# Attention in a hybrid diffusion layer: where the softmax sums' reciprocals are multiplied in

## The chip, the cores and the metric

The kernel runs on one core of a Trainium2 chip. The time is what the device needs for one execution of the whole program (two layers), in microseconds (us); lower is better. The time shown is the median of three runs. Beside it stands one profiled execution, whose trace gives the start and the duration of each instruction. TensorE does the matrix products, VectorE (DVE in the rows) the elementwise work with two operands and the reductions, ScalarE (ACT) the activations and copies, GpSimd (POOL) a few subtractions, SyncE (SP) issues most DMAs.

## The reference

Two layers over 512 latent tokens and 256 context tokens of width 1024: layer 0 mixes tokens by attention and a short convolution, layer 1 by a state-space scan; each is followed by a feed-forward block. What the change touches is the attention of layer 0, with 8 heads:

```python
def _attend(qn, qr, kn, kr, v):
    s = einsum('bqhd,bkhd->bhqk', qn, kn) + einsum('bqhr,bkr->bhqk', qr, kr)
    p = softmax(s.astype(float32) * MLA_SCALE, axis=-1).astype(v.dtype)
    return einsum('bhqk,bkhd->bqhd', p, v)
```

Latent queries see all 768 keys, context queries the 256 context keys. A value vector has 64 numbers. Everything is float32.

## The kernel before, in words

To keep float32 accuracy with TensorE's fast format (float32r), an operand is split into a rounded part (hi) and the rest (lo). A product of two such operands is three matrix products (hi·hi, hi·lo, lo·hi; the helper `mm3`).

The attention works on 24 units: 8 heads times 3 parts. Parts 0 and 1 are 256 latent queries each against 768 keys, part 2 is the 256 context queries against 256 keys. Per unit there are two functions.

`scores(h, part, q)` (lines 743 to 763): TensorE makes the scores of two tiles of 128 queries into three PSUM banks. VectorE takes the negated row maxima (line 755, one reduction over both tiles). ScalarE takes the exponentials with that as bias, and their row sums (line 758). VectorE takes the sums' reciprocals `ri`, two columns of 128 numbers (line 760), and then multiplies each tile of exponentials by its column, in place (line 762, seen in the trace at the helper's line 107).

`values(h, part, p)` (lines 765 to 793): in three steps (one for part 2), TensorE transposes four 128x128 pieces of `p` into one of two PSUM banks (`tr`, line 139), ScalarE copies them as hi into a ring of three SBUF buffers (line 783), VectorE writes the rest as lo (line 784), and TensorE multiplies the values with hi and lo into the bank `po` (lines 788 and 789). `V` holds hi and lo of the values side by side, so `po` has the hi part in partitions 0 to 63 and the lo part in 64 to 127. At the end ScalarE copies the lower half of `po` to SBUF, and VectorE adds the two halves into `m32`:

```python
t = O32()
self.act(t[0:64], po[64:128], AF.Copy)
self.tt(m32[sl, part * 256:(part + 1) * 256], po[0:64], t[0:64], ALU.add)
```

`po` is a ring with a single place, PSUM bank 5: the value products of the next unit write the same bank. `m32` gathers two heads, and is split again for the output projection (lines 812 to 814).

The loop (lines 801 to 815) makes the scores two units ahead: while `values` of unit u runs, `scores` of unit u+2 is under way. In between stand the projection of the next head's queries (`q_head`, line 732, whose VectorE part is a product of 128x768) and of the keys of the next two heads. The order of instructions on each engine is not written by hand: a planner lays out the program by its own timeline of what is ready when, and on the chip each engine then works through its queue in that order. Semaphores hold an instruction until what it reads is written and what it overwrites has been read. After the attention come the splits of the convolution's results, the output projection (line 864 on) and the feed-forward block.

Of the kernel before, what the change touches and what calls it, by code (L numbers as in the profile page):

```python
# [11 lines left out]
AF = mybir.ActivationFunctionType  # L12
ALU = mybir.AluOpType
# [80 lines left out]
class Kern:  # L94
# [358 lines left out]
    def mixer0(self):  # L453
# [12 lines left out]
        m32 = b(NT)  # L466
# [108 lines left out]
        for f in range(8):  # L575
# [10 lines left out]
            if f in (3, 4):  # L586
                t = f + 1
# [83 lines left out]
        t = tmp()  # L671
# [5 lines left out]
        for e in range(2):  # L677
            sl = slice(64, 128) if e == 0 else slice(0, 64)
# [6 lines left out]
        for j in range(4):  # L685
# [5 lines left out]
            u = tmp()  # L691
# [14 lines left out]
        PS, PQ, PO, PTp = Ring(psa, [0], 1536), Ring(psa, [1536], NT), Ring(psa, [2560], 512), Ring(psa, [3072, 3584], 512)  # L706
# [12 lines left out]
        def key_proj(p):  # L719
            w = self.loadw(io["uk"][p], 256, WK)  # L720
            ps = PQ()
            self.gemm_fm(ps, w, ck, nk=2)
            k32 = K32()
            self.act(k32, ps, AF.Copy)
            return k32

        def key_rows(k32, e):
            sl = slice(0, 64) if e == 0 else slice(64, 128)
            self.act(Kp[e][0][sl], k32[sl], AF.Copy)
            self.tt(Kp[e][1][sl], k32[sl], Kp[e][0][sl], ALU.subtract, eng=nc.gpsimd)  # L730

        def q_head(h):
            w = self.loadw(io["uq"][h], 384, WQ)
            ps = PQ()
            self.gemm_fm(ps, w, cq, nk=3)
            q32 = Q32()
            self.tt(q32, ps, Geff[h % 2], ALU.mult)
            q = Q()
            self.act(q[:, :NT], q32, AF.Copy)
            self.tt(q[:, NT:], q32, q[:, :NT], ALU.subtract, eng=nc.gpsimd)  # L740
            return q[:, :NT], q[:, NT:]

        def scores(h, part, q):

            kp = Kp[h % 2]
            n = NT if part < 2 else NC
            ps = PS(2 * n)
            for i in range(2):
                t = 2 * part + i
                a = [q[j][:, t * 128:(t + 1) * 128] for j in range(2)]  # L750
                for c0, c1 in (SEGS if i == 0 else SEGS[::-1]) if part < 2 else (CTX,):
                    o = i * n + (c0 - (NT - n) if i == 0 or part == 2 else (c0 - NL if c0 else NC))
                    self.mm3(ps[:, o:o + c1 - c0], a, [kp[j][:, c0:c1] for j in range(2)], True, True)
            nm, sm, ri = self.small(2), self.small(2), self.small(2)
            nc.vector.tensor_reduce(out=nm, in_=ps.rearrange("p (i n) -> p i n", i=2), axis=AX.X, op=ALU.max, negate=True)
            p = Pr(2 * n)
            for i in range(2):
                self.act(p[:, i * n:(i + 1) * n], ps[:, i * n:(i + 1) * n], AF.Exp, bias=nm[:, i:i + 1],
                         accum_out=sm[:, i:i + 1])
            nc.vector.reciprocal(ri, sm)  # L760
            for i in range(2):
                self.ts(p[:, i * n:(i + 1) * n], p[:, i * n:(i + 1) * n], ri[:, i:i + 1])
            return p

        def values(h, part, p):
            n = NT if part < 2 else NC
            po = PO(256)
            kts = range(6) if part < 2 else (4, 5)

            def col(i, kt):  # L770

                if part == 2:
                    return i * n + (kt - 4) * 128
                return i * n + (kt * 128 if i == 0 else ((kt - 4) * 128 if kt >= 4 else NC + kt * 128))
            for kk in range(0, len(kts), 2):
                pt = PTp()
                for k in range(2):
                    for i in range(2):
                        c = col(i, kts[kk + k])
                        self.tr(pt[:, k * 256 + i * 128:k * 256 + (i + 1) * 128], p[:, c:c + 128])  # L780
                hl = PT()
                hi, lo = hl[:, :512], hl[:, 512:]
                self.act(hi, pt, AF.Copy)
                self.tt(lo, pt, hi, ALU.subtract)
                for k in range(2):
                    kt = kts[kk + k]
                    v = V[kt][:, h * 128:(h + 1) * 128]
                    self.mm(po, v, hi[:, k * 256:(k + 1) * 256], kt == kts[0], False)
                    self.mm(po, v, lo[:, k * 256:(k + 1) * 256], False, kt == kts[-1])
            t = O32()  # L790
            sl = slice(0, 64) if h % 2 == 0 else slice(64, 128)
            self.act(t[0:64], po[64:128], AF.Copy)
            self.tt(m32[sl, part * 256:(part + 1) * 256], po[0:64], t[0:64], ALU.add)

        k32 = key_proj(0)
        qs = {0: q_head(0)}
# [1 line left out]
        key_rows(k32, 1)  # L798
        units = [(h, part) for h in range(8) for part in range(3)]
        prob = {u: scores(0, u, qs[0]) for u in range(2)}  # L800
        for u, (h, part) in enumerate(units):
            if part == 0 and h + 1 < 8:
                qs[h + 1] = q_head(h + 1)
            if part == 1 and h % 2 == 1 and h < 7:
                k32 = key_proj((h + 1) // 2)
                key_rows(k32, 0)
            if u + 2 < len(units):
                prob[u + 2] = scores(*units[u + 2], qs[units[u + 2][0]])
            if part == 1 and h % 2 == 1 and h < 7:
                key_rows(k32, 1)  # L810
            values(h, part, prob.pop(u))
            if part == 2 and h % 2 == 1:
                self.act(mixA[0][h // 2], m32, AF.Copy)
                self.tt(mixA[1][h // 2], m32, mixA[0][h // 2], ALU.subtract, eng=nc.gpsimd)
                self.tap("attn", m32, h // 2)
# [862 lines left out]
```

## Time and profile before

| | |
|---|---|
| Time, median of 3 runs | 1946.99 us (1946.28 to 1947.25) |
| Profiled execution: its own time | 1947.97 us |
| Profiled execution: span from first to last instruction | 1946.2 us, 25422 instructions |
| TensorE busy | 1840.2 us (95%) |
| VectorE busy | 1285.7 us (66%) |
| ScalarE busy | 865.3 us (44%) |
| GpSimd busy | 472.2 us (24%) |
| Mean granted TensorE clock | 0.982 of 2.4 GHz |

The profiled execution's own time is 1.8 us longer than its span (what lies before the first and behind the last instruction), and 1.0 us longer than the median of the runs. In a row of the trace, `128x768 f32<-128x768 f32 x32 | 25.6, 843` means 32 instructions with this output and input, 25.6 us busy in all and 843 ns each in the mean. In a timeline, a row begins with start and duration in us, instructions of one kind that follow each other are merged (x4), and a bracket gives the idle time of the engine just before and what ended it. TensorE's matrix products overlap in its pipeline: one that lasts 272 ns can follow the one before it after 109 ns.

### The profile page before, as it was taken

The numbers are of one execution on the slowest core, as the hardware profiler recorded it, in microseconds if no ns is written. First come the engines' busy times: TensorE is split into PE (matmuls) and PEld (weight loads), VectorE is DVE, ScalarE is ACT, GpSimd is POOL, SyncE is SP. The second block draws the span as 40 slices with busy tenths as digits, with TensorE's granted clock in tenths as the row PEclk, the third lists the DMA queues.
The fourth block names the chain that finished last, engine by engine and source line by source line (L and its number), as shares of the span: only waits on it lengthen the run. The fifth ranks groups of instructions, "written<-read, shape, count | busy, mean of one in ns | idle before, by whom it ended". The sixth has DMA issues, their size and how long they took to land. (4 is left out here: it accounts for less than half of the span.)

```text
span 1946.2 us, 25422 instructions
## 1 busy us (share of the span) xinstructions
PE 1840.2 (95%) x9752; PEld 1549.7 (80%) x9752; DVE 1285.7 (66%) x1859; ACT 865.3 (44%) x1346; POOL 472.2 (24%) x578
## 2 busy tenths in 40 slices
PE   7999998889999999999978999999999899999997
PEld 3787787778888888888857887887778788888886
DVE  3332378746999988767666688877776266555564
ACT  4422376645534334334444556565562254333332
POOL 1000124112011111111151367777674110000002
PEclk9899999999999999999998999999999999999999
DMA  8145300153888989877662434444477963223222
GB/s 320 61 153 178 95 25 12 34 174 108 291 307 314 331 325 350 303 257 241 235 252 92 171 124 158 152 168 169 144 262 291 351 214 105 76 97 98 98 87 76
DMA packets 84034, 355.13 MB, mean 182 GB/s; under 512 B 10828, under 2 KB 13320, under 8 KB 66760
## 3 DMA queue, kind: packets, MB, share of 16 engines
q1 hardware_dynamic: 67560, 264.63, 38.0%
q0 software_dynamic: 16352, 88.87, 13.3%
q8 instruction: 77, 1.26, 0.3%
q14 instruction: 45, 0.37, 0.1%
HBM read 277.28 MB, written 76.18 MB: 182 GB/s over the span
## 5 line engine op out<-in xcount | busy, mean ns | idle before, releaser
L131 PE MATMUL psum<-arena_r 128*128 128x512 f32 (+1 forms) x8876 | 1752.8, 357 | 47.8 <-DVE arena_f L113 14.6
L131 PEld LDWEIGHTS psum<-arena_r 128*128 128x128 f32 x8876 | 1466.5, 190 | 306.6 <-ACT arena_r L101 21.9
L113 DVE TENSOR_TENSOR arena_r<-arena_f,arena_r 128x512 fp32r<-128x512 f32 (+5 forms) x417 | 388.6, 948 | 278.2 <-ACT arena_r L101 276.1
L101 ACT ACTIVATE arena_r<-arena_f 128x1024 fp32r<-128x1024 f32 (+5 forms) x465 | 344.7, 765 | 432.4 <-PE psum L131 151.0
L113 POOL TENSOR_TENSOR arena_f<-arena_f 128x256 f32<-128x256 f32 (+6 forms) x344 | 323.6, 966 | 200.2 <-ACT arena_f L101 83.0
L101 ACT ACTIVATE arena_f<-arena_f 128x512 f32<-128x512 f32 (+7 forms) x203 | 160.5, 806 | 274.0 <-DMA ws_dram<-arena_f 101.3
L110 DVE SCALAR_TENSOR_TENSOR arena_f<-psum,arena_f 128x511 f32<-128x511 f32 (+1 forms) x356 | 217.9, 649 | 64.6 <-ACT arena_f L101 61.4
L113 DVE TENSOR_TENSOR arena_f<-psum,arena_f 64x256 f32<-64x256 f32 (+6 forms) x277 | 174.8, 647 | 99.5 <-PE psum L131 82.8
L101 ACT ACTIVATE arena_f<-psum,arena_f 128x768 f32<-128x768 f32 (+2 forms) x201 | 153.6, 771 | 112.8 <-PE psum L131 58.8
L113 DVE TENSOR_TENSOR arena_f<-arena_f 128x512 f32<-128x512 f32 (+5 forms) x189 | 161.3, 865 | 48.5 <-ACT arena_f L101 33.1
L107 POOL TENSOR_SCALAR arena_f<-arena_f 128x1 f32<-128x1 f32 (+2 forms) x88 | 34.1, 388 | 558.4 <-ACT junk L101 455.9
L204 POOL DMA_DIRECT2D ws_dram<-arena_f x57 | 31.3, 548 | 459.3 <-DVE arena_f L113 361.4
L139 PE MATMUL psum<-arena_f 128*128 128x128 f32 x596 | 96.4, 285 | 45.5 <-DVE arena_f L107 30.2
L101 ACT ACTIVATE arena_f<-psum 128x512 f32<-128x512 f32 (+9 forms) x152 | 80.7, 549 | 105.2 <-PE psum L131 91.9
L139 PEld LDWEIGHTS psum<-arena_f 128*128 128x128 f32 x596 | 71.3, 143 | 64.6 <-DVE arena_f L107 35.9
L113 POOL TENSOR_TENSOR arena_r<-arena_f,arena_r 128x768 fp32r<-128x768 f32 (+2 forms) x28 | 50.1, 1803 | 247.2 <-ACT arena_r L101 232.5
L110 DVE SCALAR_TENSOR_TENSOR arena_f<-arena_f 128x512 f32<-128x512 f32 (+4 forms) x107 | 70.9, 701 | 53.7 <-ACT arena_f L101 45.3
L317 DVE SCALAR_TENSOR_TENSOR junk<-arena_f 128x1024 bf16<-128x1024 f32 x80 | 97.5, 1219 | 1.9 <-DMA arena_f<-in_mod_t_dram 1.5
L101 ACT ACT_TABLE_LOAD x51 | 65.4, 1283 | 34.6 <-DVE arena_f L110 18.8
L107 DVE TENSOR_SCALAR arena_f<-arena_f 128x512 f32<-128x512 f32 (+4 forms) x97 | 55.2, 612 | 29.2 <-POOL arena_f L113 28.5
L101 ACT ACTIVATE arena_r<-psum 128x512 fp32r<-128x512 f32 (+2 forms) x72 | 41.1, 591 | 28.2 <-PE psum L139 14.3
L113 DVE TENSOR_TENSOR arena_r<-psum,arena_r 128x512 fp32r<-128x512 f32 (+2 forms) x72 | 47.4, 674 | 9.0 <-ACT arena_r L101 8.7
(29 smaller groups left out, 300.6 us busy)
## 6 DMA issues: line engine op xcount, KB each, us to landing
arena_r<-ws_dram SPq DMA_DIRECT2D x64, 1024.0 KB
ws_dram<-arena_f POOLq DMA_DIRECT2D x56, 1024.0 KB, 5.2
arena_f<-in_ffn_up_dram SPq DMA_DIRECT2D x88, 512.0 KB
arena_f<-in_mod_t_dram SPq DMA_DIRECT2D x56, 512.0 KB
arena_f<-in_ffn_down_dram SPq DMA_DIRECT2D x44, 512.0 KB
arena_f<-in_mod_dram SPq DMA_DIRECT2D x40, 512.0 KB
arena_f<-a_dram SPq DMA_DIRECT2D x32, 512.0 KB
arena_f<-in_ssd_w_dram POOLq DMA_DIRECT2D x24, 512.0 KB, 7.1
```

The costliest lines, as they stand in the source:

```text
L101: return self.nc.scalar.activation(out=out, in_=in_, func=func, **kw).ins
L107: (eng or self.nc.vector).tensor_scalar(**kw)
L110: self.nc.vector.scalar_tensor_tensor(out=out, in0=in0, scalar=s, in1=in1, op0=op0, op1=op1)
L113: return (eng or self.nc.vector).tensor_tensor(out=out, in0=a, in1=b, op=op).ins
L131: self.nc.tensor.matmul(out, a, b, start=start, stop=stop)
L139: self.nc.tensor.transpose(out, in_, self.ident)
L204: g.dma_start(out=self.wsd[i * 128:(i + 1) * 128, :2 * n], in_=hl)
L317: self.nc.vector.scalar_tensor_tensor(out=self.junk2, in0=r, scalar=1.0, in1=self.cb[c], op0=ALU.mult, op1=ALU.mult, accum_out=o)
```

## The change

`scores` no longer multiplies the exponentials by `ri`; it hands `ri` on. `values` multiplies the exponentials as they are. Behind the value products, TensorE makes two more products per unit, in float32 (not float32r): a column of `ri`, repeated 64 times as the stationary operand, times the 128x128 identity. This writes `ri` of 128 queries as a row, on 64 partitions, into the second half of the bank `po` (columns 256 to 511). The sum of the two halves of the value product now goes to SBUF, and another VectorE instruction of 64x256 multiplies it by these rows into `m32`.

```diff
             nc.vector.reciprocal(ri, sm)
-            for i in range(2):
-                self.ts(p[:, i * n:(i + 1) * n], p[:, i * n:(i + 1) * n], ri[:, i:i + 1])
-            return p
+            return p, ri
 
-        def values(h, part, p):
+        def values(h, part, p, ri):
             n = NT if part < 2 else NC
-            po = PO(256)
+            po = PO(512)
...
-                    self.mm(po, v, hi[:, k * 256:(k + 1) * 256], kt == kts[0], False)
-                    self.mm(po, v, lo[:, k * 256:(k + 1) * 256], False, kt == kts[-1])
+                    self.mm(po[:, :256], v, hi[:, k * 256:(k + 1) * 256], kt == kts[0], False)
+                    self.mm(po[:, :256], v, lo[:, k * 256:(k + 1) * 256], False, kt == kts[-1])
+            for i in range(2):
+                self.mm(po[0:64, 256 + i * 128:256 + (i + 1) * 128], ri[:, i:i + 1].to_broadcast([128, 64]), self.ident, True, True)
             t = O32()
             sl = slice(0, 64) if h % 2 == 0 else slice(64, 128)
-            self.act(t[0:64], po[64:128], AF.Copy)
-            self.tt(m32[sl, part * 256:(part + 1) * 256], po[0:64], t[0:64], ALU.add)
+            self.act(t[0:64], po[64:128, :256], AF.Copy)
+            self.tt(t[0:64], po[0:64, :256], t[0:64], ALU.add)
+            self.tt(m32[sl, part * 256:(part + 1) * 256], po[0:64, 256:], t[0:64], ALU.mult)
...
-            values(h, part, prob.pop(u))
+            values(h, part, *prob.pop(u))
```

## Rows read from the trace of the kernel before

**Rows 1.** The page: busy time of each engine over the whole span, share and instructions.

```profile
PE 1840.2 (95%) x9752; PEld 1549.7 (80%) x9752; DVE 1285.7 (66%) x1859; ACT 865.3 (44%) x1346; POOL 472.2 (24%) x578
```

**Rows 2.** Three stretches of the attention: start and end and length in us, then busy us and instructions of TensorE's products, its weight loads, VectorE, ScalarE and GpSimd, the granted TensorE clock, the DMA share and GB/s.

```profile
235.00:295.00 60.00, 57.09 (x369) 50.37 (x368) 46.13 (x74) 39.98 (x81) 17.85 (x10) 1.00 0.09 29
295.00:394.00 99.00, 83.43 (x547) 71.71 (x545) 80.33 (x123) 65.44 (x138) 28.16 (x16) 1.00 0.10 29
315.00:375.00 60.00, 49.86 (x331) 43.09 (x329) 53.54 (x76) 42.39 (x89) 22.84 (x13) 1.00 0.06 19
```

**Rows 3.** What TensorE's products waited for between 235 and 394 us: tile and line, us in total, times, longest.

```profile
PE psum L139 <- DVE arena_r L113: 6.1, 8, 1.5
PE psum L131 <- DVE arena_f L113: 4.5, 4, 1.3
PE psum L139 <- DVE arena_f L107: 3.3, 3, 1.5
PE psum L131 <- DVE arena_r L113: 3.1, 3, 1.4
```

**Rows 4.** VectorE between 235 and 394 us, by line and shape: busy us, mean ns, and the idle time before.

```profile
L755 DVE TENSOR_REDUCE arena_f<-psum 128x2 f32<-128x1536 f32 x16 | 28.0, 1751 | 1.7 <-PE psum L131 1.5
L107 DVE TENSOR_SCALAR arena_f<-arena_f 128x768 f32<-128x768 f32 x32 | 25.6, 843 | 0.4
L113 DVE TENSOR_TENSOR arena_f<-psum,arena_f 64x256 f32<-64x256 f32 x24 | 9.9, 414 | 3.9 <-ACT arena_f L101 3.5
L107 DVE TENSOR_SCALAR arena_f<-arena_f 128x256 f32<-128x256 f32 x16 | 8.8, 593 | 0.1
```

**Rows 5.** TensorE over the whole span, by line and shape (arena_r holds float32r, arena_f float32): busy us, mean ns of one, idle time before.

```profile
L131 PE MATMUL psum<-arena_r 128*128 128x512 f32 x5724 | 1370.1, 395 | 24.1 <-DMA arena_r<-ws_dram 8.4 <-ACT arena_r L101 6.8 <-DVE arena_f L113 6.2
L131 PE MATMUL psum<-arena_r 128*128 128x256 f32 x3056 | 425.9, 288 | 23.8 <-DVE arena_f L113 8.4 <-DVE arena_r L113 7.7 <-ACT arena_r L101 3.9
L131 PE MATMUL psum<-arena_f 128*128 128x512 f32 x2 | 1.0, 590 | 0.0
L131 PE MATMUL psum<-arena_f 128*128 128x256 f32 x2 | 0.6, 378 | 0.0
```

**Rows 6.** Timeline of VectorE and TensorE around 302 us: a reduction of two tiles' scores, and transposes with what they wait for.

```profile
301.26 1.74 DVE L755 TENSOR_REDUCE arena_f<-psum 128x2 f32<-128x1536 f32 x1
302.17 0.60 PE L139 MATMUL psum<-arena_f 128*128 128x128 f32 x4
303.66 0.66 PE L139 MATMUL psum<-arena_f 128*128 128x128 f32 x4 [0.89 <-DVE arena_r L113]
```

**Rows 7.** Timeline around 327 us: the multiplications of line 107, GpSimd beside them, and TensorE.

```profile
325.37 2.71 DVE L107 TENSOR_SCALAR arena_f<-arena_f 128x768 f32<-128x768 f32 x2
325.79 3.99 POOL L113 TENSOR_TENSOR arena_r<-arena_f,arena_r 128x768 fp32r<-128x768 f32 x2 [0.74 <-ACT arena_r L101]
328.13 0.55 PE L139 MATMUL psum<-arena_f 128*128 128x128 f32 x3 [1.44 <-DVE arena_f L107]
```

**Rows 8.** Timeline around 307 us: the same multiplications with GpSimd idle, and TensorE, waiting for the lo part that follows them.

```profile
306.20 1.14 DVE L107 TENSOR_SCALAR arena_f<-arena_f 128x768 f32<-128x768 f32 x2
308.00 0.66 PE L139 MATMUL psum<-arena_f 128*128 128x128 f32 x4 [0.59 <-DVE arena_r L113]
```

**Rows 9.** Six more of TensorE's waits between 236 and 394 us, from its timeline in order of time.

```profile
272.51 0.66 PE L139 MATMUL psum<-arena_f 128*128 128x128 f32 x4 [0.64 <-DVE arena_r L113]
297.18 0.65 PE L139 MATMUL psum<-arena_f 128*128 128x128 f32 x4 [0.70 <-DVE arena_r L113]
323.17 1.55 PE L131 MATMUL psum<-arena_r 128*128 128x256 f32 x10 [1.22 <-DVE arena_f L113]
352.34 0.74 PE L131 MATMUL psum<-arena_r 128*128 128x256 f32 x4 [1.33 <-DVE arena_r L113]
368.77 0.75 PE L131 MATMUL psum<-arena_r 128*128 128x256 f32 x4 [1.43 <-DVE arena_r L113]
392.06 0.73 PE L131 MATMUL psum<-arena_r 128*128 128x256 f32 x4 [1.33 <-DVE arena_f L113]
```

**Rows 10.** VectorE's timeline at three places, around 271, 294 and 321 us: multiplications, a lo part (128x512), and the sum of the two halves (64x256).

```profile
270.11 1.15 DVE L107 TENSOR_SCALAR arena_f<-arena_f 128x768 f32<-128x768 f32 x2
271.77 0.68 DVE L113 TENSOR_TENSOR arena_r<-psum,arena_r 128x512 fp32r<-128x512 f32 x1
...
291.42 2.84 DVE L107 TENSOR_SCALAR arena_f<-arena_f 128x256 f32<-128x256 f32 x2
...
316.68 3.12 DVE L107 TENSOR_SCALAR arena_f<-arena_f 128x768 f32<-128x768 f32 x2
322.69 0.42 DVE L113 TENSOR_TENSOR arena_f<-psum,arena_f 64x256 f32<-64x256 f32 x1
```

**Rows 11.** VectorE's timeline from 349 to 367 us: the first and the last of three places (at 349, 355 and 366 us) at which the sum of the two halves stands ahead of a reduction of 128x1536 and this ahead of lo parts.

```profile
349.48 0.42 DVE L113 TENSOR_TENSOR arena_f<-psum,arena_f 64x256 f32<-64x256 f32 x1
349.93 1.76 DVE L755 TENSOR_REDUCE arena_f<-psum 128x2 f32<-128x1536 f32 x1
...
...
366.36 1.76 DVE L755 TENSOR_REDUCE arena_f<-psum 128x2 f32<-128x1536 f32 x1
```

**Rows 12.** The end of the attention: the last sum, and TensorE, which starts on it.

```profile
393.56 0.42 DVE L113 TENSOR_TENSOR arena_f<-psum,arena_f 64x256 f32<-64x256 f32 x1
394.03 1.47 PE L131 MATMUL psum<-arena_r 128*128 128x512 f32 x3 [1.24 <-DVE arena_f L113]
```

## The prediction

> **What bounds the kernel now.** I read the page first: TensorE is busy 95% of the span [rows 1], so a change in a stage counts only by what it adds to TensorE's queue or takes from its waits. The change lies between 235 and 394 us. In that stage the clock is 1.00 throughout, so nothing is to be had from it, and it has two halves [rows 2]. From 235 to 295 us TensorE is busy 57.1 of 60 us, 95%, with VectorE at 46.1 of 60, 77%. From 315 to 375 us VectorE has risen to 53.5 of 60, 89%, and TensorE fallen to 49.9, 83%. The waits name the partner: all 17.0 us that TensorE's products wait in the stage (6.1 + 4.5 + 3.3 + 3.1) are waits for VectorE [rows 3]. So there is something to win, 17 us at the utmost, 0.9% of the time.
>
> The kind of wait matters more. Three waits, 3.3 us, are for the removed multiplications themselves (line 107) [rows 3]: one is 1.44 us, where two multiplications beside a busy GpSimd take 2.71 us [rows 7] and not 1.14 us as with GpSimd idle [rows 8]. Eleven waits, 9.2 us, are for a lo part (6.1 + 3.1) [rows 3], and what the lo part itself queued behind must be read from VectorE's timeline. Sometimes it is a multiplication [rows 8]; oftener it is the row maxima's reduction, 1.74 us: at 302 us TensorE has filled both transpose banks, the lo part that would free one starts only when the reduction that began at 301.26 ends, and TensorE stands 0.89 us [rows 6]. The reduction stays.
>
> **The change part by part.**
>
> Removed: 32 multiplications of 128x768 (25.6 us) and 16 of 128x256 (8.8 us), 34.4 us of VectorE [rows 4]. Off TensorE's waits this takes: the three for line 107, 3.3 us; the two lo waits that stand right behind multiplications, 0.64 us at 272 and 0.59 us at 308 [rows 8 to 10]. That is 4.5 us, and I count it whole. At two more places multiplications stand further up the chain. Before 323 us 3.12 us of them push two lo parts, these a reduction, and it the sum for which TensorE waits 1.22 us; at 297 us it waits 0.70 us behind such a chain, which begins with 2.84 us [rows 9, 10]. The reduction cannot begin before its scores are made, so I take half of these 1.92 us, 1.0 us. Sum: -5.5 us. The lower bound is the 3.3 us alone; the upper one all of the 17 us.
>
> Added to TensorE: 48 products of 128 columns with 64 stationary columns, in plain float32. The trace has none of this shape. By the rows for float32r, 256 more columns cost 395 - 288 = 107 ns; for float32 590 - 378 = 212 ns [rows 5]: two clocks of 2.4 GHz per column where float32r takes one. So 128 columns need 107 ns. The transposes, also float32 with 128 columns, follow each other after (0.60 - 0.27)/3 = 0.11 us, four in 0.60 us with a last one of 0.27 us [rows 6]. I take 0.11 us each, 0.22 us per unit, 5.3 us for 24 units. Nothing says that a stationary operand which repeats one column loads slower. Bounds: nothing where TensorE would stand anyway, and twice the price if such a load is as slow as a float32 product of 256 columns (215 ns), 10.5 us.
>
> What of the 5.3 us is hidden: where a lo part is held up by a reduction that already runs, 0.22 us more on TensorE ends inside the wait. Of the eleven lo waits two go with the multiplications; I count the nine others, most of which stand behind a reduction, with 0.22 us each, 2.0 us. The other 3.3 us are on the path: in the first half TensorE is 95% busy, and a product there is paid in full. The two products also stand ahead of ScalarE's copy of half of `po`, if the bank is guarded as a whole, and behind that copy in ScalarE's queue wait the next hi parts; these depend on transposes that TensorE issues behind the two products anyway, so this is the same 0.22 us and not a second one. The products wait for `ri`, which has been ready for the better part of two units.
>
> Added to VectorE: 24 multiplications of 64x256 with one operand in PSUM. The sum of the halves has this shape and takes 414 ns [rows 4], so 24 x 0.414 = 9.9 us; VectorE is relieved of 34.4 - 9.9 = 24.5 us net. On the path this instruction counts in two ways. First, `po` is now read 0.41 us longer, and the next unit's value products wait for it: TensorE waits for the sum three times, first at 323 and last at 392 us [rows 9], and three times 0.41 is 1.2 us. Secondly, behind the sum in VectorE's queue stands a reduction and behind that the lo part that TensorE awaits; that is so three times, ahead of the first wait at 352 and of the last at 368 us [rows 9, 11], again 1.2 us. In the other units the multiplication falls into VectorE's own slack. Bounds: nothing, and all 9.9 us.
>
> At the end of the attention copy, sum and output projection follow each other with TensorE idle 1.24 us [rows 12]; the last unit's 0.22 + 0.41 us come on top there. The 0.22 is in the 3.3; I add 0.4 us.
>
> Sum: -5.5 + 3.3 + 1.2 + 1.2 + 0.4 = +0.6 us. No DMA is added, removed or passed, and what follows the attention is TensorE's own queue, so a shift at 394 us is handed on to the end. Against the profiled execution's own 1947.97 us this gives 1948.6; the runs' median is 1.0 us lower, so 1947.6. The halves and shares in this sum are worth some 3 us either way, and VectorE's net relief of 24.5 us, which I have booked only at named waits, leans to the faster side: I put the forecast at 1947.0 us, no change. Its own range is 1943.5 to 1950.5.
>
> **A rule that speaks against the change.** By the rows a float32 product takes two clocks per column [rows 5]. The Trainium skill, page "FP8 and Floating Point Precision", section "TensorE Precision Notes", says that true float32 takes four passes through the array. By that the 48 products would cost 48 x 0.213 = 10.2 us instead of 5.3. The trace does not agree with it for the two shapes that it has, and the sum goes by the trace.
>
> **The rivals.**
>
> *Faster: VectorE is what sets the pace of the second half.* Then the relief is not worth single waits but the pace: with VectorE back below 77% TensorE works the second half as densely as the first. From 295 to 394 us it is busy 83.4 of 99 us [rows 2]; 14 units add 14 x 0.22 = 3.1; at 95.2% this takes 90.9 us, 8.1 less. The first ten units lose 10 x 0.22 = 2.2. That makes -5.9 us, 1941.1. For it: all waits name VectorE, and GpSimd stretches the multiplications most in this half [rows 2, 7]. Against: the reduction, 1.75 us each and 16 times [rows 4], stays in the same queue ahead of the lo parts.
>
> *Slower: the end of a unit becomes the chain.* Two products, copy, sum and multiplication must be over before the next unit's value products may write `po`, and the reduction queues behind them. If that decides in 12 of 24 units, the multiplication costs 12 x 0.41 = 5.0, the products are paid in full, 5.3, and the gain is the same -5.5: +4.8 us, 1951.8. It decides from about ten units on. For it: TensorE already waits for the sum, and a bank with one place leaves no way around. Against: only three such waits in 24 units (the fourth wait for VectorE's arena_f at line 131 is for a head's queries) [rows 3, 9].
>
> *Slower: the new products cost twice.* If repeated columns load slowly, or this shape takes four clocks per column, TensorE gets 10.5 us, and the sum is 0.6 + 5.2 = +5.8 us, 1952.8. The rows speak against it [rows 5].
>
> That the change does not do what it says I leave out: the instructions are plainly removed and added. What is open is the planner: with other durations it orders the stage anew, which can move any of these waits by a microsecond or two; this widens the ranges.
>
> **How the numbers follow.** What a measurement of this kernel can tell from no change is about 0.2%, 3.9 us. Chances: forecast 0.46, faster rival 0.31, end of the unit 0.18, dear products 0.05. The forecast's range lies within 3.9 us of the time before, so the chances are faster 0.31, same 0.46, slower 0.23. The range reaches into both sides: down to 1939.0, two below the faster rival (of the 17 us all but a few could go), up to 1954.0, where both slower cases with some of the planner's own are inside.
>
> **What would show it.** In the trace after, line 107 is gone between 235 and 394 us, and TensorE has no wait for it; that stage's VectorE busy time falls by about 24 us. The two products show as pairs 0.11 us apart. Right is the forecast if the lo waits behind reductions remain, about 8 us, and waits for the new multiplication at `po` appear. Wrong on the fast side: TensorE's busy share from 315 to 375 us rises to 95%. Wrong on the slow side: waits of the value products for VectorE's 64x256 in ten units or more, or pairs 0.2 us apart and more.

## The result and the profile after

The change makes the kernel slower by 0.6%: 1959.26 us in the median (1955.01 to 1962.57, four runs) against 1947.12 us (1946.28 to 1948.58) beside it, a ratio of 1.0059, 95% interval 1.0046 to 1.0071. That is 12.1 us, outside the range of 1939 to 1954. The profiled execution after is the quickest of the four, 1955.01 us, so its trace can show only some 7 us of the loss.

The first line of the page after answers to [rows 1]:

```profile
PE 1851.2 (95%) x9848; PEld 1554.1 (80%) x9848; DVE 1265.5 (65%) x1835; ACT 869.9 (45%) x1350; POOL 471.4 (24%) x578
```

TensorE has 11.0 us and 96 instructions more, where 48 products were added. The same three stretches of the attention as in [rows 2], with the same columns:

```profile
235.00:295.00 60.00, 57.55 (x375) 50.09 (x374) 38.76 (x60) 37.80 (x78) 13.55 (x8) 1.00 0.09 27
295.00:394.00 99.00, 93.53 (x614) 79.27 (x613) 60.55 (x103) 64.30 (x135) 28.66 (x17) 1.00 0.07 22
315.00:375.00 60.00, 56.73 (x374) 47.78 (x372) 39.80 (x66) 40.79 (x85) 20.87 (x13) 1.00 0.06 18
```

VectorE is at 38.8 and 60.6 us in the first two, before at 46.1 and 80.3; TensorE is at 94% of the second, before at 84%, and at 95% from 315 to 375 us, which the prediction had named as the sign of a faster kernel. The stage still ends later: busier TensorE here means more work, not the same work done sooner. What TensorE waited for from 235 us to 402 us, where the attention and its tail now end (tile and line; us, times, longest), answers to [rows 3]:

```profile
PE psum L131 <- DVE arena_f L113: 5.8, 5, 1.5
PE psum L131 <- DVE arena_r L113: 3.4, 4, 1.4
PE psum L131 <- ACT arena_f L101: 0.7, 2, 0.4
PE psum L139 <- DVE arena_r L113: 0.6, 2, 0.3
PE psum L131 <- ACT arena_r L101: 0.3, 1, 0.3
```

The sum is 10.8 us against 17.0. Line 107 is gone, the waits for a lo part (arena_r) fell from 9.2 to 4.0 us, those for arena_f (the sum, now with the multiplication behind it, and a head's queries) rose from 4.5 to 5.8. VectorE by shape in that stretch, for [rows 4]:

```profile
L755 DVE TENSOR_REDUCE arena_f<-psum 128x2 f32<-128x1536 f32 x16 | 28.0, 1753 | 8.3 <-PE psum L131 8.1
L113 DVE TENSOR_TENSOR arena_f<-psum,arena_f 64x256 f32<-64x256 f32 x48 | 20.0, 416 | 10.0 <-ACT arena_f L101 9.1
```

The multiplication costs what the sum does, 416 ns. The reduction had waited 1.7 us for its scores in all and now waits 8.3: VectorE is ahead of TensorE. And the new products, by shape from 235 to 402 us:

```profile
L131 PE MATMUL psum<-arena_f 128*64 128x128 f32 x96 | 15.6, 285 | 0.0
```

and in two places of TensorE's timeline:

```profile
308.55 0.65 PE L131 MATMUL psum<-arena_f 128*64 128x128 f32 x4
309.13 0.66 PE L139 MATMUL psum<-arena_f 128*128 128x128 f32 x4
...
315.05 0.65 PE L131 MATMUL psum<-arena_f 128*64 128x128 f32 x4
315.63 4.69 PE L131 MATMUL psum<-arena_r 128*128 128x512 f32 x25
```

A unit asks for two products; TensorE executes four instructions, and the next one starts 0.58 us after the first (309.13 - 308.55, 315.63 - 315.05). One by one, the starts follow after 0.159, 0.109, 0.109 and 0.203 us (medians of the 24 units).

To see where along the program the time goes, I cut each trace at TensorE's own products, what an edit added not counted: the start of the 1000th (attention), the 2400th (first feed-forward block), the 5250th (scan layer), the 8250th (second feed-forward block). Lengths of before and differences to them, in us, for all kernels:

```
                       start  attention  ffn0   scan   ffn1
before                 185.2    264.4   532.1  607.6  338.4
after                   -3.4     +6.1     0.0   +4.2    0.0
e1_no_products          -3.4     +0.9     0.0   +6.2    0.0
e2_rows_by_transpose    -1.6     -0.7     0.0   +0.1    0.0
e3_products_twice       -2.3    +14.3     0.0   +3.6    0.0
e4_products_only        -1.8    +17.6     0.0   +9.3    0.0
e5_relief_only          -3.5     -3.2     0.0   +6.7    0.0
e6_rows_own_bank        -0.5    +11.0     0.0   -1.1    0.0
e7_barrier_before       -0.8      0.0     0.0   +6.0    0.0
e8_barrier_after        -0.2     +6.0     0.0   +9.0    0.0
e9_before_nudged        -2.6     +0.2    +0.4   +0.6    0.0
e10_after_nudged        -3.0     +5.9     0.0   +1.6    0.0
e11_scale_on_gpsimd     -2.4    +13.2    +2.2   -4.3    0.0
```

The start, which no edit touches, differs from one execution to the next by up to 3.5 us; the granted clock of the first 100 us is 0.93 in the mean before and 0.95 after, which may be part of it. The change costs +6.1 us in the attention and, some 500 us later, +4.2 us in the scan layer, where not one instruction was edited. e9 and e11 have 4 and 20 idle transposes in the first feed-forward block, which are its +0.4 and +2.2.

How far may such a column be trusted? In the attention, TensorE works through its instructions in e7 and e9 in the order of before, in e8 and e10 in the order of after: 0.0 and +0.2, +6.0 and +5.9 beside +6.1, so the same order repeats within 0.2 us. Every other kernel has its own order there, since the planner lays out the stage anew. e2 is closest to after, with 56 of the 1400 products moved (by line, tiles and shape; counted as the fewest that must move); between before and after it is 165, and e1, e3, e4, e5, e6 and e11 are 128 to 229 away from the kernel that they edit. Of the experiments on the attention, e2 is thus the cleanest; the others change the order along with what they are meant to change.

### The profile page after: what moved, and what is told of

Same layout as the page of the kernel before. It is cut to its first block, busy times and chain, and to the rows that moved or that the text cites. A ratio compares the mean times of both kernels' runs of the same rounds, so it can differ in the third digit from the quotient of the medians.

```text
span 1953.2 us, 25617 instructions
## 1 busy us (share of the span) xinstructions
PE 1851.2 (95%) x9848; PEld 1554.1 (80%) x9848; DVE 1265.5 (65%) x1835; ACT 869.9 (45%) x1350; POOL 471.4 (24%) x578
## 4 chain that ended last, share of the span: by engine, by line
PE 40%; issue 20%; DVE 9%; DMA 4%; POOL 3%; ACT 3%; SPq 0%; DVEq 0%; POOLq 0%; ACTq 0%
PE psum L131 39%; DVE arena_f L113 3%; DVE arena_r L113 3%; POOL arena_f L113 3%; DVE arena_f L110 2%; DMA arena_f<-a_dram 1%; DMA arena_r<-ws_dram 1%; ACT arena_f L101 1%; PE psum L139 1%; DVE arena_f L1355 1%; ACT L101 1%; DMA ws_dram<-arena_f 1%; ACT arena_r L101 1%; POOL arena_f L107 0%; DMA g_dram<-arena_f 0%
## 5 line engine op out<-in xcount | busy, mean ns | idle before, releaser
L101 ACT ACTIVATE arena_f<-arena_f 128x768 f32<-128x768 f32 (+7 forms) x203 | 160.1, 806 | 257.9 <-DMA ws_dram<-arena_f 95.2
L113 DVE TENSOR_TENSOR arena_f<-psum,arena_f 64x256 f32<-64x256 f32 (+5 forms) x301 | 185.1, 629 | 110.0 <-PE psum L131 86.0
L131 PE MATMUL psum<-arena_f 128*32 128x512 f32 (+5 forms) x370 | 57.4, 442 | 1.8 <-ACT arena_f L101 1.2
```

The costliest lines, as they stand in the source:

```text
L101: return self.nc.scalar.activation(out=out, in_=in_, func=func, **kw).ins
L113: return (eng or self.nc.vector).tensor_tensor(out=out, in0=a, in1=b, op=op).ins
L131: self.nc.tensor.matmul(out, a, b, start=start, stop=stop)
```

## The experiments

Two questions: what costs the 6 us in the attention (the price of the products, or the end of a unit, or a relief that is worth less than thought), and what costs the 4 us in the scan layer (a new order that the planner gives it, or something else). Ratios are to the kernel before, run beside each, with 95% intervals.

**e1, no products** (1952.07 us, 1.0039 [1.0026, 1.0052]):

```diff
-            for i in range(2):
-                self.mm(po[0:64, 256 + i * 128:256 + (i + 1) * 128], ri[:, i:i + 1].to_broadcast([128, 64]), self.ident, True, True)
...
-            self.tt(m32[sl, part * 256:(part + 1) * 256], po[0:64, 256:], t[0:64], ALU.mult)
+            self.tt(m32[sl, part * 256:(part + 1) * 256], po[0:64, :256], t[0:64], ALU.mult)
```

> The changed kernel without its 96 float32 products: the rows of reciprocals are not made, the last multiplication takes the first half of the bank instead, so the normalisation is left out; all else of the change stays. Theory P (the products' price: each shows as two instructions, some 0.12 us each, 0.5 us per unit, 12 us in all): the attention, which took 6.2 us longer than before, falls to 4 to 6 us shorter than before. Rival U (the end of the unit: the added VectorE multiplication and the longer hold on the bank): the attention stays at least 3 us longer than before. For the layer with the scan (4.2 us longer after the change, its instructions in a new order) theory O (the planner's order) says that it moves by some us whenever the order there is new, whatever the attention does; here the order is new.

The attention came out at +0.9, between what the two theories allow: 5.2 us below after, yet no gain on before. TensorE's waits from 225 to 392 us:

```profile
PE psum L131 <- DVE arena_f L113: 8.7, 8, 1.8
PE psum L131 <- ACT arena_f L101: 5.8, 6, 2.0
PE psum L139 <- DVE arena_r L113: 5.2, 6, 1.5
PE psum L131 <- DVE arena_r L113: 0.8, 1, 0.8
```

Eight waits for arena_f, where after has four in this stretch: part of the products' place is taken by waits. One of them on VectorE's and on TensorE's timeline:

```profile
346.08 0.41 DVE L113 TENSOR_TENSOR arena_f<-psum,arena_f 64x256 f32<-64x256 f32 x1
346.41 1.74 DVE L755 TENSOR_REDUCE arena_f<-psum 128x2 f32<-128x1536 f32 x1
348.07 0.41 DVE L113 TENSOR_TENSOR arena_f<-psum,arena_f 64x256 f32<-64x256 f32 x1
```

```profile
348.63 1.07 PE L131 MATMUL psum<-arena_r 128*128 128x256 f32 x7 [1.75 <-DVE arena_f L113]
```

The sum ends at 346.5, but VectorE's queue has the reduction between sum and multiplication; `po` is free only at 348.5, and the next value products wait 1.75 us. That is the rival of the unit's end, dearer in one place than its 0.41 us, and in fewer places.

**e2, rows by transposes** (1943.99 us, 0.9990 [0.9981, 0.9999]; eleven runs):

```diff
-                self.mm(po[0:64, 256 + i * 128:256 + (i + 1) * 128], ri[:, i:i + 1].to_broadcast([128, 64]), self.ident, True, True)
+                self.tr(po[0:64, 256 + i * 128:256 + (i + 1) * 128], ri[:, i:i + 1].to_broadcast([128, 64]))
```

> The changed kernel with the rows of reciprocals made by TensorE's transposes (48 instructions) in place of float32 products (96). Theory P: the attention falls by 5 to 6 us against the changed kernel, to within 1 us of before. Rival U: it stays at least 4 us longer than before, since bank, copy, sum and multiplication are the same. Theory O: the planner's order in the scan layer is here as before on TensorE but for one place, so that layer takes as long as before within 1 us. By P and O the whole is at 1946 to 1949 us.

As theory P has it: the same rows from the same operand, in nearly the same order, and the attention is at -0.7, 6.8 us less than after; the whole is 2 us quicker than expected. TensorE by shape from 225 to 410 us:

```profile
L139 PE MATMUL psum<-arena_f 128*64 128x128 f32 x48 | 9.1, 271 | 0.0
```

48 instructions instead of 96, with the same 64 stationary columns and 128 columns, 0.108 us from one start to the next. So it is not the repeated column and not the narrow operand that is dear, but the product in float32. With the price that I had assumed (0.22 us per unit) the change is what I had forecast for it, no change within 0.2%. The faster rival priced the products at 0.22 us too and put the attention at -5.9; it does not come out.

**e3, each product twice** (1963.64 us, 1.0088 [1.0074, 1.0102]):

```diff
-            for i in range(2):
+            for i in (0, 1, 0, 1):
```

> The changed kernel with each float32 product issued twice (192 instructions, the same result). Theory P: the attention grows by another 10 to 12 us, to 16 to 18 us longer than before. Rival U: the products are not what counts, and it grows by 4 us at most.

The attention takes 8.2 us more than after (14.3 - 6.1), under the 10 to 12 expected and under 24 x 4 x 0.109 = 10.5 us, but twice what the rival allows: more products cost most of their time, which speaks for TensorE as the bound of the stage at the margin.

**e4, the products alone** (1971.35 us, 1.0132 [1.0119, 1.0145]): the kernel before, with the products of the change added to it and unused.

```diff
-            return p
+            return p, ri
...
-            po = PO(256)
+            pq = PO(512)
+            po = pq[:, :256]
...
+            for i in range(2):
+                self.mm(pq[0:64, 256 + i * 128:256 + (i + 1) * 128], ri[:, i:i + 1].to_broadcast([128, 64]), self.ident, True, True)
```

> The kernel before with the products added alone, into the unused half of the bank: the exponentials are multiplied as before, nothing reads the rows. Theory P: the attention is 8 to 12 us longer than before (a little may hide in TensorE's 17 us of waits). Rival U: 3 us at most, since no multiplication is added at the end of the unit.

More than expected, +17.6 us in the attention. Its waits from 225 to 410 us:

```profile
PE psum L131 <- DVE arena_f L113: 13.0, 8, 3.2
PE psum L131 <- ACT arena_f L101: 1.6, 3, 0.9
```

With the multiplications still in VectorE's queue the waits for arena_f stand at 13.0 us. Beside e4 the change's relief is worth 17.6 - 6.1 = 11.5 us; beside e5, next, without the products, 3.2 us. So the relief has no size of its own that would hold in every order; what it is worth depends on what stands beside it.

**e5, relief alone** (1948.68 us, 1.0017 [1.0007, 1.0027]): the kernel before without line 762.

```diff
-            for i in range(2):
-                self.ts(p[:, i * n:(i + 1) * n], p[:, i * n:(i + 1) * n], ri[:, i:i + 1])
```

> The kernel before without its 48 multiplications of the exponentials and with nothing in their place (the normalisation is left out). The forecast booked 5.5 us for this relief. Theory E (the relief is real, and what the first experiment lost again was lost at the end of the unit, where a reduction stands in VectorE's queue between the sum and the new multiplication while the bank is held): the attention is 4 to 8 us shorter than before. Rival N (VectorE's relief is worth nothing, TensorE's waits only change their names): within 2 us of before.

34.4 us of VectorE removed and nothing put in their place give 3.2 us in the attention: TensorE's idle time from the 1000th to the 2400th product only falls from 23.1 to 22.0 us. That lies between what theory E (4 to 8 us) and rival N (within 2 us) expected. So VectorE's busy time as such does not set the pace of the stage, which with e2 speaks against the faster rival. The whole kernel is even slower, by its scan layer, +6.7.

**e6, rows in a bank of their own** (1957.03 us, 1.0052 [1.0037, 1.0066]): e2 with the rows outside `po`.

```diff
+        RO = Ring(psa, [2304], 256)
...
-            po = PO(512)
+            po, rows = PO(256), RO(256)
...
+                self.tr(rows[0:64, i * 128:(i + 1) * 128], ri[:, i:i + 1].to_broadcast([128, 64]))
...
+            self.tt(m32[sl, part * 256:(part + 1) * 256], rows[0:64], t[0:64], ALU.mult)
```

> As the second experiment (rows of reciprocals by 48 transposes), but the rows go to the free half of another PSUM bank (bank 4), so the value products of the next unit wait only for the sum, as before the change, and no longer for the new multiplication. Theory E: TensorE's waits for VectorE's arena_f at line 131 in the attention, 8.9 us there, fall to 5 us or less, and the attention gains 3 to 5 us on that experiment, to about 4 us shorter than before; the whole 1939 to 1942 us. Rival N: the multiplication off the bank changes nothing, attention within 1.5 us of that experiment's. The planner's order in the scan layer is here as before on TensorE, so that layer takes as long as before within 1 us.

A miss by 15 us: +11.0 in the attention. TensorE's timeline repeats its waits every 40.1 us:

```profile
249.36 0.74 PE L131 MATMUL psum<-arena_r 128*128 128x256 f32 x4 [1.05 <-DVE arena_r L113]
257.51 0.74 PE L131 MATMUL psum<-arena_r 128*128 128x256 f32 x4 [1.34 <-DVE arena_r L113]
...
282.39 3.02 PE L131 MATMUL psum<-arena_r 128*128 128x512 f32 x12 [1.65 <-DVE arena_f L113]
289.50 0.74 PE L131 MATMUL psum<-arena_r 128*128 128x256 f32 x4 [1.05 <-DVE arena_r L113]
297.67 0.74 PE L131 MATMUL psum<-arena_r 128*128 128x256 f32 x4 [1.34 <-DVE arena_r L113]
...
322.50 3.02 PE L131 MATMUL psum<-arena_r 128*128 128x512 f32 x12 [1.65 <-DVE arena_f L113]
```

Here the planner laid out the whole stage in another, periodic order, with 25.2 us of waits from 235 to 405 us. So this run says nothing about sharing the bank `po`. That the order is what costs the 10 us and more is likely but not shown: the rows also moved into a bank that the projections of keys and queries use.

**e7 and e8, a barrier of all engines ahead of the scan layer**, in the kernel before (1954.14 us, 1.0042 [1.0030, 1.0054]) and after (1962.90 us, 1.0080 [1.0068, 1.0093]). Both then have one order of instructions in the scan layer.

```diff
+            tc.strict_bb_all_engine_barrier()
             self.mixer1()
```

> The kernel before with a barrier of all engines ahead of the scan layer, which makes the planner lay out that layer from the same state whatever the attention was. It is the base for the next one; the barrier costs some us, the same in both.

> The changed kernel with the same barrier; from the barrier on the instructions stand in the same order as in the kernel before with the barrier. Theory O (4 us of the loss come from the planner's new order in the scan layer): that layer takes the same time in both within 0.5 us, and the whole differs by the attention's share alone, 5 to 7 us. Rival: the scan layer suffers from something else that the change brings (the place where the attention ends, DMAs that come later); then it is still about 4 us longer, and the whole differs by 9 to 12 us.

With the order the same, the distance of the two traces is +6.3 us at the 5000th product and +6.2 at the 7840th, at 1526 us; nine tenths of the products between them lie within 5.7 to 6.9. The attention's +6.0 is carried through, and nothing is added in some 500 us of scan layer. The 3 us by which the table's scan column still differs (9.0 and 6.0) arise at one place behind that. Ten us of e7 and the same ten of e8 (columns as in [rows 2]):

```profile
1530.00:1540.00 10.00, 7.66 (x34) 6.03 (x33) 0.00 (x0) 0.00 (x0) 0.00 (x0) 1.00 0.98 381
1536.30:1546.30 10.00, 6.29 (x26) 4.84 (x25) 0.00 (x0) 0.00 (x0) 0.00 (x0) 0.86 0.94 352
```

In e8 the granted clock is 0.86 of 2.4 GHz in the mean, with a stretch at 1.2 GHz from 1543.6 us on, while TensorE stood waiting 3.71 us for weights; in e7 it waits 2.34 us at that place and the clock is 1.00. The order is the same there, so this is something else. It may not be chance either: the medians are 8.8 us apart, more than the attention's 6.0, and lie between the 5 to 7 us of theory O and the 9 to 12 of its rival. What makes these last 3 us stays open.

**e9 and e10, idle instructions added.** A few idle instructions ahead of the first feed-forward block, in before and in after, meant to make the planner lay the rest out anew: e9 1948.35 us, 1.0006 [0.9995, 1.0017]; e10 1950.97 us, 1.0023 [1.0012, 1.0034], twelve runs each.

```diff
+            for _ in range(4):
+                self.tr(self.T(128), self.ident)
             self.ffn(0)
```

```diff
+            for _ in range(10):
+                self.nc.vector.memset(self.junk2, 0.0)
             self.ffn(0)
```

> The kernel before with four idle transposes of the identity (0.4 us of TensorE) between the attention's layer and its feed-forward block, and nothing else. They make the planner lay out the scan layer in another order, much as after the change. Theory O: the attention takes as long as before within 1 us, the scan layer 3 to 8 us longer, the whole 1949 to 1954 us, though next to nothing was added. Rival (the order is without effect, the changed kernel's scan layer suffers from something that comes with the change itself): the scan layer within 1 us of before, the whole within 1.5 us.

> The changed kernel with ten idle VectorE memsets ahead of the first feed-forward block, with which the planner lays out the scan layer in the same order as in the kernel before. Theory O: the scan layer is back within 1 us of before, the attention stays about 6 us longer, the whole at 1951 to 1954 us. Rival: the scan layer stays about 4 us longer, the whole at 1957 to 1961 us.

e10 has the attention of after (+5.9) and the scan layer's order of before: its scan stage is at +1.6, and the whole loss shrinks from 12.1 us to 4.1 (1950.97 - 1946.84). e9 did not become the test that it was meant to be: the order of its scan layer is that of before but for eight of 3000 places on TensorE, the same as in e2, and not one close to that of after. With the order kept, its scan stage is at +0.6, so it only shows that the idle instructions themselves cost nothing there.

**e11, the multiplications on GpSimd** (1958.77 us, 1.0062 [1.0045, 1.0079]): the kernel before, line 762 with GpSimd as its engine, and twenty idle transposes ahead of the feed-forward block.

```diff
+            for _ in range(20):
+                self.tr(self.T(128), self.ident)
             self.ffn(0)
...
-                self.ts(p[:, i * n:(i + 1) * n], p[:, i * n:(i + 1) * n], ri[:, i:i + 1])
+                self.ts(p[:, i * n:(i + 1) * n], p[:, i * n:(i + 1) * n], ri[:, i:i + 1], eng=nc.gpsimd)
```

> The kernel before with the 48 multiplications of the exponentials moved to GpSimd, which is busy some 48 of 167 us there; and 20 idle transposes (2.2 us) ahead of the first feed-forward block, which keep the scan layer in the order of the kernel before. It relieves VectorE by 34 us without a product on TensorE. Theory E (VectorE's relief takes TensorE's idle time in the attention from 23 to some 15 us as in the changed kernel): the attention 4 to 8 us shorter, the whole 1940 to 1944 us. Rival G (GpSimd is too slow, and its subtractions for queries and keys come late): the attention as long as before or longer.

The attention is at +13.2. GpSimd by shape, and what that makes of TensorE's waits, both from 225 to 405 us:

```profile
L107 POOL TENSOR_SCALAR arena_f<-arena_f 128x768 f32<-128x768 f32 x32 | 70.6, 2218 | 18.8 <-DVE arena_f L762 17.0 <-PE psum L139 1.7
```

```profile
PE psum L139 <- DVE arena_r L113: 12.3, 11, 2.2
PE psum L131 <- ACT arena_f L101: 5.3, 7, 1.3
```

A multiplication takes 2.2 us there, 0.57 us on an undisturbed VectorE [rows 8]; the lo parts come later for it.

## Why the prediction was wrong

**The relief (-5.5 us): right in place, its size borne out only by the whole stage.** Line 107's 3.3 us are gone, the lo waits fell by 5.2 us, where I had booked 1.23 + 1.0 for the multiplications and 2.0 us for products hidden in them. By waits named in the profile, the stage went from 17.0 to 10.8 us, by -6.2; my terms for waits make -5.5 - 2.0 + 1.2 + 1.2 = -5.1. No run fixes the relief by itself: without the products 3.2 us come of it (e5), beside them 11.5 (e4), each in an order of its own.

**The price of the products (5.3 us): the step that failed.** It is 24 x 0.58 = 13.9 us from the first product's start to the next instruction, and up to 16 us with the gap ahead of the first (0.21 us, in e2 0.12). The pairs that were to be 0.11 us apart are 0.27 us apart (0.159 + 0.109), past the 0.2 us that I had named as the sign of being wrong. The working took two clocks per column from 590 - 378 ns and treated this as the whole product. But [rows 5] count x2 for 128x512 and x2 for 128x256 in float32, and the kernel asks for one of each there (line 676 makes one product per segment): each record is half a product. Two records of 0.109 us make 0.218 us per product, 10.5 us for 48, twice my figure; the rest, 3.4 us and more (up to 5.6 with the gap ahead), is lost on going into and out of float32 products (0.159 and 0.203 us instead of 0.109). I had also written that the trace did not agree with the four passes of the Trainium skill, page "FP8 and Floating Point Precision", section "TensorE Precision Notes". It does agree: two instructions of two clocks per column are four. The estimate of 10.2 us worked out from it would have been close to the 10.5 us that the records give; the switching is in neither. The dear-products rival, to which I gave 0.05, had the right mechanism in its second condition, four clocks per column; e2 speaks against its first, the repeated column. That its +5.8 us meets the attention's +6.1 is in part luck: it lacked the switching, and TensorE's idle time shrank by 8.5 us where my terms have 5.1.

The sum of the attention with this term corrected: waits -6.2, products +13.9 to +16.1, that is +7.7 to +9.9 against +6.1 measured. By TensorE's whole idle time between the 1000th and the 2400th product (23.1 us before, 14.6 after, -8.5) it is +5.4 to +7.6, which holds it.

**The multiplication at `po` and ahead of reductions (+1.2, +1.2): the first about right, the second not seen by itself.** 416 ns as taken; the waits for arena_f rose by 1.3 us, with one wait more. What the multiplication adds to lo waits behind a reduction has no row of its own; these waits fell in all. The rival of the unit's end would have needed ten such waits, and there are five at most; e1 shows that it is real where TensorE has less to do.

**"A shift at 394 us is handed on to the end", and a planner that moves waits "by a microsecond or two": failed too.** Through the first feed-forward block it holds (0.0 in every row of the table but the two with transposes added there). In the scan layer the planner, which works with its own times, gave the same instructions another order. Compared in TensorE's sequence there, e4 is the same as after, and e1 and e5 are but for a few instructions: +9.3, +6.2, +6.7, after +4.2. e6 and e10 have the sequence of before, and e2, e9 and e11 have it but for eight places: -1.1, +1.6, +0.1, +0.6, -4.3. (e3, +3.6, has one of its own.) These are single executions, and within one order they spread by 5 to 6 us, but the two groups do not overlap. Nor do they in the medians: take the attention (and the added transposes) off each kernel's distance to before, and what is left is +6.0 for after, +5.5, +8.1 and +5.9 for e1, e4 and e5, and -1.0, 0.0, +0.9, -1.8 and -3.5 for e2, e6, e9, e10 and e11. Where a barrier fixed the order, nothing was added over some 500 us, and 3 us behind that. Part of it is seen in TensorE's waits in the scan layer, before from 1060 to 1490 us:

```profile
PE psum L131 <- DVE arena_f L113: 8.9, 11, 2.3
PE psum L131 <- ACT arena_r L101: 7.8, 10, 1.3
PE psum L139 <- ACT arena_f L101: 3.9, 1, 3.9
```

and after from 1063 to 1497 us:

```profile
PE psum L131 <- DVE arena_f L113: 11.1, 12, 2.3
PE psum L131 <- ACT arena_r L101: 9.1, 10, 2.1
PE psum L139 <- ACT arena_f L101: 5.0, 3, 3.7
PE psum L139 <- DVE arena_f L113: 3.0, 3, 2.5
```

The growth is 2.2 + 1.3 + 1.1 + 3.0 = 7.6 us in these rows; of the others two grow by 1.5 together and one shrinks by 1.8. I could not name one instruction whose new place is to blame.

**In all:** some 6 us from the attention and 4 to 7 from the scan layer make 10 to 13 us; the measurement says 12.1. **Open** are what the change would cost in the attention at a fixed order (before and after differ in it, and e6 suggests that another order can be worth 10 us), so how much of e2's -0.7 is the change and how much luck of the order, and what makes the last 3 us of e8. e2 is the only version that beats both kernels, by 0.1%, an interval that barely excludes 1.

## What to carry to other kernels

Before pricing an operation from a row, compare the row's count with the number of such operations in the code: a float32 product stands in the trace as two instructions, and the step from one of them to the next is half its price. To turn a column into rows use a transpose, which is one. And where a planner or compiler orders the program, an edit can move the time in a layer that it does not touch: cut both traces at the same instructions, compare the sequences, and try another order before crediting a few microseconds to the edit.

## What the runs showed that I had not expected

- A float32 product with 64 stationary and 128 moving columns is two instructions 0.109 us apart; the float32 transpose of the same shape is one. Two products take 0.58 us from the first to the next instruction, two transposes 0.22.
- Changing from float32r to float32 products and back cost 0.09 us behind the last float32r product (0.21 instead of 0.12), 0.05 after the first float32 one and 0.09 after the last, in every unit (the last one where no wait follows); transposes show no such gap.
- The same scan layer took 4.2 to 9.3 us more than before with its instructions in the order of after (four kernels), and from 4.3 less to 1.6 more in the order of before (five kernels).
- In the attention, one order of instructions repeated its time within 0.2 us from one execution to the next; a kernel with another order there is not compared as sharply.
